# A delay in the written order for the small matmuls of the weight chains, and priority for the reductions behind them

## The chip, the cores and the metric

The kernel runs on 1 core of one Trainium2 chip. The metric is device microseconds of one execution, as the median of several runs. The core has five engines that are met here: TensorE (PE in the profile; its weight loads are PEld), VectorE (DVE), ScalarE (ACT), GpSimd (POOL) and SyncE (SP), which issues most DMAs. Each executes its own list of instructions in order, and semaphores tie the lists together.

## The reference, cut to what matters

A trunk of two layers over 2048 tokens plus 16 meta tokens of width 1024, in float32. Each layer is one input projection, attention in two groups of 8 heads, a gate, an output projection, and a layer norm of the residual sum:

```
x <- LayerNorm(alpha * x + (concat(heads_a, heads_b) * silu(gate)) @ w_out)
layer 0: stick-breaking attention (8 heads)  ||  multi-head latent attention (8 heads, rotary key)
layer 1: sliding-window attention with sinks ||  forgetting attention (8 heads)
stick-breaking: w[q,k] = exp(log_sigmoid(z[q,k]) + sum of log_sigmoid(-z[q,j]) over k < j < q)
```

The kernel works with pairs of float16 numbers (a high and a low part) in place of float32. To split a tensor that way it needs a power of two as its scale, and for the scale the largest absolute value of the tensor. To scale the mixed outputs it also needs bounds, and for those the largest norm of a column (of x and of some weights).

## The kernel before

**Stages.** Stick-breaking attention for 4 pairs of heads comes first, then latent attention for 4 pairs, the first output projection with its layer norm, forgetting attention for 4 pairs, sliding-window attention for 4 pairs, and the second output projection. Tokens are handled in 4 blocks of 512 and in tiles of 128. For each pair and block, a group of P blocks projects k, q, v and gate (`mm3` at L825 for k and q, `proj_4` at L915 for v and gate, `proj_tok` at L888 for the meta tokens). A blocks do the attention of a tile: scores by `qk` (L1087) into two PSUM banks, the softmax or the stick-breaking scans (L1415, L1417) and products (L1431), a split into high and low (L1205, L1218), a transpose by DMA (L588), the product with v (L1278 to L1280) into `psO`, and the multiplication with gate and factor (L1364 in the stick-breaking attention). F blocks do the output projections.

**The order.** The order of all instructions is written when the program is built, by a small event simulation (`Flow`). It has a clock `t`, a priority queue for each engine, and events. `f.job(engine, ns, fn, then, pr)` queues a step with an assumed duration; when the engine is free in the simulation, the job with the smallest `pr` is taken and `fn` writes its instructions; `then` is called after the duration and an assumed latency. Without `pr`, the priority is the time of queueing. `EARLY` and `LATE` are 3000 ns each: `f.t - EARLY` goes ahead of what has been waiting for less than that, `f.t + LATE` yields. `f.at(lag, fn)` calls `fn` after `lag` ns of simulated time. TensorE's queue (`"P"`) is emptied whenever the drive loop comes back to it, before the next few projection or score matmuls. On the chip, each engine executes what was written, in that order, whenever its operands are there.

**The weight chains.** `prep` loads a group of weights (two staging buffers, `wst`), takes the largest absolute value of each partition (L698), and calls `allreduce` for the largest over all partitions: VectorE writes a diagonal matrix of the 128 values (L626), TensorE multiplies it with ones (L631) so that each partition gets all values, VectorE reduces them (L634). The result becomes the scale (L86 to L90), and the group is split (L655 on ScalarE, L653 on VectorE or L645 and L646 on GpSimd) into one of four weight buffers (`wg`). For v and gates, `maxnorm` follows: squares (L755, on GpSimd, or for the parts of x mostly on VectorE), a matmul with ones that sums them (L760), a copy into a column (L781, L783), `allreduce`, and a square root (L790). The squares have one buffer (`nsq`), which is given back in `red`, right after the matmul has been placed. The norm of x takes 17 parts of up to 128 tokens through that buffer, one after the other; the norms of v and g of the first pair stand behind them in the same queue.

**What waits for the results.** A projection waits for its split weights. A norm group's weight buffer is given back when its norm is known. In the stick-breaking attention `pr.fm`, which L1364 needs, is computed when the norms of x, v and g are there (`units` in `phase_sb`). PSUM has 6 banks for scores and projections, at most 4 of them for scores, reductions and norms together ("S"); scores of a tile take two at once, and start when two are to be had. `psO` has two more buffers.

Of the kernel before, what the change touches and what calls it, by code (L numbers as in the profile page):

```python
# [16 lines left out]
ALU = mybir.AluOpType  # L17
AX = mybir.AxisListType
PSUM = bass.MemoryType.PSUM

D = 1024
# [18 lines left out]
EARLY, LATE, SLACK = 3000.0, 3000.0, 5000.0  # L40
XPOOL = (1, 4, 6)
NEGD = True
SWABIAS = 0.0
LOBIAS = 1000.0
MORE = ()
WGS = 4
SB_BYTES, MLA_ROWS, FOX_ROW = 204768, 24704, 8256
# [357 lines left out]
def dve(n):  # L405
    return 1.042 * n + 69.0


def gps(n):
    return 1.88 * n + 150.0  # L410
# [15 lines left out]
class Kern:  # L426
# [189 lines left out]
    def allreduce(self, m, then, pr=None):  # L616


        nc, f = self.nc, self.f
        r = self.small.tile([128, 1], F32, name="amr", tag="amr")  # L620

        def diag():
            d = self.small.tile([128, 128], BF16, name="amd", tag="amd", bufs=2)

            def fn():
                nc.vector.tensor_scalar(d, self.idbf, m, 1.0 + 2.0 ** -8, ALU.mult, ALU.mult)  # L626

            f.job("D", 190.0, fn, lambda: self.bk.get(lambda ps: ones(d, ps)), pr)

        def ones(d, ps):  # L630
            f.job("P", 60.0, lambda: nc.tensor.matmul(ps[:, :128], lhsT=self.ones, rhs=d, start=True, stop=True), lambda: red(ps), pr)  # L631

        def red(ps):
            f.job("D", dve(128), lambda: nc.vector.tensor_reduce(r, ps[:, :128], axis=AX.X, op=ALU.max), lambda: [self.bk.free("S", ps), then(r)], pr)  # L634

        diag()

# [103 lines left out]
    def maxnorm(self, parts, g, after=None, facs=None):  # L741


        nc, f = self.nc, self.f
        mx = self.small.tile([128, 24], F32, name="nmx", tag="nmx", bufs=3)
        left = [len(parts)]

        def one(i, sq):
            src = parts[i]
            k, n = src.shape[1], src.shape[2]  # L750
            if len(parts) > 1 and i % 3:
                e, ns, eng = "D", dve(k * n / 2), nc.vector
            else:
                e, ns, eng = "G", gps(k * n), nc.gpsimd
            f.job(e, ns, lambda: eng.tensor_tensor(sq[:, :k, :n], src, src, ALU.mult), lambda: self.bk.get(lambda ps: mm(i, k, n, sq, ps)), f.t + LATE)  # L755

        def mm(i, k, n, sq, ps):
            def fn():
                for kt in range(k):
                    nc.tensor.matmul(ps[:n, 0:1], lhsT=sq[:, kt, :n], rhs=self.ones[:, 0:1], start=kt == 0, stop=kt == k - 1)  # L760

            f.job("P", k * 28.0, fn, lambda: red(i, n, ps, sq))

        def red(i, n, ps, sq):
            self.nsq.free(sq)

            def end():
                self.bk.free("S", ps)
                left[0] -= 1
                if left[0]:  # L770
                    return
                if len(parts) > 1:
                    f.job("D", 90.0, lambda: nc.vector.tensor_reduce(mx[:, 23:24], mx[:, :len(parts)], axis=AX.X, op=ALU.max), lambda: self.allreduce(mx[:, 23:24], root))
                else:
                    self.allreduce(mx[:, 0:1], root)

            def fn():
                if n < 128:
                    nc.vector.memset(mx[:, i:i + 1], 0.0)
                if facs:  # L780
                    nc.vector.tensor_scalar(mx[:n, i:i + 1], ps[:n, 0:1], facs[i][:n], facs[i][:n], ALU.mult, ALU.mult)  # L781
                else:
                    nc.vector.tensor_copy(mx[:n, i:i + 1], ps[:n, 0:1])  # L783

            f.job("D", 140.0 if facs else 70.0, fn, end)

        r = self.small.tile([128, 1], F32, name="nr", tag="nr")

        def root(m):
            f.job("G", 460.0, lambda: nc.gpsimd.tensor_tensor(r, m, self.half, ALU.pow), fin)  # L790

        def fin():
            def fn():
                g.nb = self.p2.mul(r, self.p2.inv(g.s), 1.02)
                g.nready = True
                if after:
                    after()
            f.job("D", 450.0, fn)

        for i in range(len(parts)):  # L800
            self.nsq.get(lambda sq, i=i: one(i, sq))
# [392 lines left out]
    def pv_hi(self, e):  # L1194
# [14 lines left out]
        def lo():  # L1209
            d, g = dve(w), gps(w)  # L1210
            if e.meta:
                d, g = d + dve(32), g + gps(32)
            onD = f.load["D"] + d + LOBIAS < f.load["G"] + g
            eng, name, ns = (nc.vector, "D", d) if onD else (nc.gpsimd, "G", g)
# [1531 lines left out]
    def phase_out0(self):  # L2746
# [5 lines left out]
        def mem():  # L2752
            wo = B(4, [2, 1024], F16)
            mt = B(2, [8, 128], F16)
            for b in MORE:
                getattr(self, b).grow(1)
# [708 lines left out]
```

## Time and profile before

| | us |
|---|---|
| median of 3 runs (3091.64 to 3104.94) | 3101.06 |
| the profiled execution, own time | 3114.27 |
| its span | 3112.2 |
| TensorE busy (34,261 matmuls) | 2608.2 (84%) |
| VectorE busy | 2439.8 (78%) |
| ScalarE busy | 1775.4 (57%) |
| GpSimd busy | 1576.6 (51%) |

The span goes from the first to the last of the 88,537 instructions in the profile. Busy shares are averages over stages with different limits, and an engine that waits for a semaphore is not busy. Times in the rows below are microseconds from the start of the span, of this one execution; "idle" of an engine is put down to the instruction that released the next one.

### The profile page before, as it was taken

How to read it: one execution, taken by the hardware profiler on the slowest of the kernel's cores; microseconds unless marked ns; L12 is line 12 of the kernel's file. 1: busy time of each engine (PE TensorE's matmuls, PEld its weight loads, DVE VectorE, ACT ScalarE, POOL GpSimd, SP SyncE). 2: the span in 40 equal slices, each digit the busy share in tenths (PEclk: the TensorE clock that was granted, in tenths of full speed). 3: DMA queues.
4: the chain of work that ended last, by engine and by line, in shares of the span. 5: the costliest groups of instructions: out<-in, count | busy, mean ns of one | idle time of the engine just before them, and what ended most of it. 6: DMA issues, size and time to landing. Idle time of an engine off the chain costs nothing. (4 is left out here: it accounts for less than half of the span.)

```text
span 3112.2 us, 88537 instructions
## 1 busy us (share of the span) xinstructions
PE 2608.2 (84%) x34261; PEld 1794.9 (58%) x34261; DVE 2439.8 (78%) x6874; ACT 1775.4 (57%) x4082; POOL 1576.6 (51%) x2292
## 2 busy tenths in 40 slices
PE   4888988888887798888776799968969797799998
PEld 2676766766775455545554355646746465566643
DVE  8889899989998786667686875866757576588866
ACT  4667677757875465556575335455465554566611
POOL 3566566755754354445465534344454443456500
PEclk9989999999998999999887899989989899899999
DMA  4365465666798699999999985777667666555863
GB/s 153 54 125 108 98 120 113 114 115 108 128 162 186 166 196 215 221 212 188 164 166 168 215 205 87 145 134 141 115 125 134 118 128 107 101 123 100 177 166 112
DMA packets 1206808, 444.62 MB, mean 143 GB/s; under 512 B 1091616, under 2 KB 1171584, under 8 KB 1206384
## 3 DMA queue, kind: packets, MB, share of 16 engines
q1 hardware_dynamic: 1204048, 430.50, 71.1%
q0 software_dynamic: 2336, 8.46, 0.8%
q8 instruction: 268, 4.39, 0.6%
q14 instruction: 156, 1.28, 0.1%
HBM read 119.62 MB, written 51.06 MB: 55 GB/s over the span
## 5 line engine op out<-in xcount | busy, mean ns | idle before, releaser
L1218 POOL TENSOR_TENSOR mem<-mem 128x512 f16<-128x512 f32 (+3 forms) x751 | 823.6, 1107 | 440.4 <-ACT mem L1205 414.1
L825 PE MATMUL bank<-mem 128*128 128x512 f16 (+2 forms) x4272 | 929.1, 369 | 8.7 <-DVE mem L1485 2.6
L1205 ACT CAST mem<-mem 128x512 f16<-128x512 f32 (+3 forms) x1080 | 520.3, 513 | 276.6 <-DMA mem<-mem 134.4
L825 PEld LDWEIGHTS <-mem 128*128 128x128 f16 (+1 forms) x4272 | 405.9, 100 | 438.6 <-issue 88.2
L1278 PE MATMUL psO<-mem 128*128 128x64 f16 x3264 | 403.8, 200 | 294.4 <-DMA mem<-mem 287.8
L915 PE MATMUL bank<-mem 128*128 128x128 f16 x9984 | 643.7, 221 | 5.5 <-DVE mem L970 4.1
L915 PEld LDWEIGHTS <-mem 128*128 128x128 f16 x9984 | 578.3, 99 | 49.4 <-issue 41.0
L1087 PE MATMUL bank<-mem 64*128 64x256 f16 (+8 forms) x6264 | 521.3, 286 | 47.4 <-DVE mem L1431 22.5
L1278 PEld LDWEIGHTS <-mem 128*128 128x128 f16 x3264 | 307.4, 101 | 426.9 <-DMA mem<-mem 367.0
L1522 ACT ACTIVATE mem<-mem,smt,p 128x656 f32<-128x656 f32 (+16 forms) x264 | 336.3, 1275 | 237.3 <-DVE smt L1519 206.7
L1280 PE MATMUL psO<-mem 128*128 128x64 f16 x3264 | 400.6, 199 | 0.0
L1279 PE MATMUL psO<-mem 128*128 128x64 f16 x3264 | 400.5, 199 | 0.0
L1087 PEld LDWEIGHTS <-mem 64*128 64x128 f16 (+1 forms) x6264 | 271.8, 96 | 195.8 <-issue 100.1
L1279 PEld LDWEIGHTS <-mem 128*128 128x128 f16 x3264 | 310.3, 102 | 15.2 <-issue 2.4
L1280 PEld LDWEIGHTS <-mem 128*128 128x128 f16 x3264 | 311.1, 102 | 0.0
L1218 DVE TENSOR_TENSOR mem<-mem 128x512 f16<-128x512 f32 (+3 forms) x329 | 254.8, 791 | 66.4 <-ACT mem L1205 62.9
L1417 DVE TENSOR_TENSOR_SCAN mem<-mem 128x513 f32<-128x513 f32 (+2 forms) x224 | 290.7, 1325 | 4.9 <-ACT mem L1407 4.6
L1550 POOL TENSOR_TENSOR ist<-ist,p 128x2 f32<-128x2 f32 (+1 forms) x196 | 49.7, 254 | 425.1 <-DVE ist L1547 406.1
L1490 DVE CUSTOM_DVE_ANT_0 mem<-bank,mem 128x256 f32<-128x256 f32 (+6 forms) x484 | 195.5, 455 | 74.2 <-PE bank L1093 48.9
L1407 ACT ACTIVATE mem<-bank,p 128x512 f32<-128x512 f32 (+3 forms) x360 | 213.1, 592 | 45.0 <-PE bank L1087 44.4
L1325 POOL TENSOR_TENSOR mem<-mem 128x128 f16<-128x128 f32 (+1 forms) x264 | 136.9, 522 | 176.1 <-ACT mem L1322 174.3
L1485 DVE TENSOR_SCALAR_CACHE_REDUCE mem<-bank 128x512 f32<-128x512 f32 (+5 forms) x372 | 188.8, 545 | 38.3 <-PE bank L1093 22.6
(191 smaller groups left out, 4130.2 us busy)
## 6 DMA issues: line engine op xcount, KB each, us to landing
mem<-in_w_dram SPq DMA_DIRECT2D x46, 512.0 KB, 4.0
tmp_mx_dram<-mem SPq DMA_DIRECT2D x128, 128.0 KB, 2.4
mem<-in_wout_dram SPq DMA_DIRECT2D x32, 512.0 KB, 4.3
mem<-mem SPq DMA_TRANSPOSE x988, 3.4
mem<-tmp_cqT_dram SPq DMA_DIRECT2D x12, 1024.0 KB, 6.5
mem<-in_xr_dram SPq DMA_DIRECT2D x16, 512.0 KB, 4.5
tmp_res_dram<-mem POOLq DMA_DIRECT2D x16, 512.0 KB, 5.0
mem<-tmp_res_dram SPq DMA_DIRECT2D x16, 512.0 KB, 5.3
```

The source lines that it names most:

```text
L825: nc.tensor.matmul(out, lhsT=st(kt, a), rhs=mv(kt, b), start=i == 0 and j == 0, stop=i == m - 1 and j == 2)
L915: nc.tensor.matmul(ps[:, 128 * i:128 * i + 128], lhsT=mv(a)[:, kt, 128 * i:128 * i + 128], rhs=w[b][:, kt, c0:c0 + 128], start=i == 0 and ...
L1087: nc.tensor.matmul(o, lhsT=l, rhs=m, start=i == 0, stop=mask is None and i == len(run) - 1)
L1205: nc.scalar.copy(t[:r, a:a + w], e.P[:r, e.pcol:e.pcol + w])
L1218: eng.tensor_tensor(t[:r, a + w:a + 2 * w], e.P[:r, e.pcol:e.pcol + w], t[:r, a:a + w], ALU.subtract)
L1278: nc.tensor.matmul(out, lhsT=p[:, a, :r], rhs=vt[:, hd, 0, :], start=e.first and i == 0 and hd == 0, stop=False)
L1279: nc.tensor.matmul(out, lhsT=p[:, a, :r], rhs=vt[:, hd, 1, :], start=False, stop=False)
L1280: nc.tensor.matmul(out, lhsT=p[:, b, :r], rhs=vt[:, hd, 0, :], start=False, stop=False)
L1407: nc.scalar.activation(b[:r, 1:n + 1], ps[:r, :n], AF.Sigmoid, scale=pr.scn[:r])
L1417: nc.vector.tensor_tensor_scan(pc[:r, :n + 1], b[:r, :n + 1], self.diag[:r, :n + 1], prev[0], ALU.mult, ALU.bypass)
L1490: nc.vector.tensor_tensor_reduce(row[:r, o + oo:o + oo + w], ps[:r, oo:oo + w], pr.cum[kb][hd][:r, ko:ko + w], 1.0, -3e38, ALU.add, ALU.ma ...
L1522: nc.scalar.activation(row[:r, :n], row[:r, :n], AF.Exp, bias=st[:r, 1:2], scale=sc[:r], accum_out=it.st[:r, hd:hd + 1])
```

## The change

Three places change. In `allreduce`, the ones matmul is asked for 2500 ns of simulated time (`PESLACK`) after its diagonal instead of at once, and so is the PSUM bank that it takes; in `maxnorm`, the norm matmul likewise after its squares. The reduction behind the ones matmul (L634) gets priority `f.t - EARLY` instead of that of its chain, and so does the copy behind the norm matmul (L781, L783), which had the time of its queueing. All callers of `allreduce` and `maxnorm` are concerned: the weights, x, the weights of latent attention and of the output projections, and the layer-norm bounds.

```diff
+PESLACK = 2500.0
...
@@ allreduce
-            f.job("D", 190.0, fn, lambda: self.bk.get(lambda ps: ones(d, ps)), pr)
+            f.job("D", 190.0, fn, lambda: f.at(PESLACK, lambda: self.bk.get(lambda ps: ones(d, ps))), pr)
...
-            f.job("D", dve(128), lambda: nc.vector.tensor_reduce(r, ps[:, :128], axis=AX.X, op=ALU.max), lambda: [self.bk.free("S", ps), then(r)], pr)
+            f.job("D", dve(128), lambda: nc.vector.tensor_reduce(r, ps[:, :128], axis=AX.X, op=ALU.max), lambda: [self.bk.free("S", ps), then(r)], f.t - EARLY)
...
@@ maxnorm
-            f.job(e, ns, lambda: eng.tensor_tensor(sq[:, :k, :n], src, src, ALU.mult), lambda: self.bk.get(lambda ps: mm(i, k, n, sq, ps)), f.t + LATE)
+            f.job(e, ns, lambda: eng.tensor_tensor(sq[:, :k, :n], src, src, ALU.mult), lambda: f.at(PESLACK, lambda: self.bk.get(lambda ps: mm(i, k, n, sq, ps))), f.t + LATE)
...
-            f.job("D", 140.0 if facs else 70.0, fn, end)
+            f.job("D", 140.0 if facs else 70.0, fn, end, f.t - EARLY)
```

## Rows read from the trace of the kernel before

**Rows 1.** Stage: busy PE, PEld, DVE, ACT, POOL (xcount), PEclk, DMA share, GB/s.

```profile
131.00:165.00 34.00, 29.86 (x415) 20.35 (x415) 31.25 (x49) 25.44 (x60) 23.80 (x23) 0.95 0.73 133
165.00:200.00 35.00, 29.81 (x505) 25.99 (x503) 29.42 (x56) 23.77 (x53) 22.63 (x23) 0.90 0.54 86
...
300.00:350.00 50.00, 47.11 (x604) 33.26 (x602) 41.04 (x89) 28.20 (x72) 24.90 (x27) 1.00 0.39 84
350.00:1000.00 650.00, 550.77 (x8537) 429.62 (x8535) 612.39 (x1002) 472.33 (x1088) 412.82 (x423) 0.97 0.69 129
...
1060.00:1630.00 570.00, 466.63 (x6145) 294.37 (x6146) 406.88 (x1346) 348.97 (x805) 297.59 (x482) 0.93 1.02 195
...
1720.00:1785.00 65.00, 49.31 (x220) 20.93 (x218) 61.90 (x107) 22.98 (x21) 44.55 (x26) 0.87 0.93 207
1785.00:1805.00 20.00, 17.20 (x90) 9.74 (x90) 10.47 (x24) 6.79 (x9) 1.49 (x2) 0.84 0.57 163
1805.00:1850.00 45.00, 42.82 (x247) 20.81 (x245) 42.17 (x96) 12.65 (x13) 24.46 (x17) 0.99 0.93 227
1850.00:2850.00 1000.00, 847.50 (x11841) 604.19 (x11839) 703.08 (x2768) 546.09 (x1308) 469.93 (x851) 0.93 0.67 122
```

**Rows 2.** Line L631: until when TensorE idled before it (us, times).

```profile
  DVE amd L626: 73.5, 30
```

**Rows 3.** TensorE waits in 0:131, 1000:1060, 1630:1720, 1720:1850, 1850:2850: us, times, longest.

```profile
PE bank L631 <- DVE amd L626: 40.3, 8, 15.1
...
PE bank L631 <- DVE amd L626: 3.0, 1, 3.0
...
PE bank L631 <- DVE amd L626: 5.9, 2, 4.3
...
PE bank L631 <- DVE amd L626: 11.8, 5, 3.0
PE bank L760 <- POOL mem L755: 4.5, 1, 4.5
...
PE psO L1278 <- DMA mem<-mem: 123.3, 82, 8.8
PE bank L631 <- DVE amd L626: 8.6, 10, 1.5
```

**Rows 4.** Timeline of TensorE, 40 to 54 us: start, us, instruction.

```profile
53.30 0.26 PE L631 MATMUL bank<-amd,ones 128*128 128x128 bf16 x1 [7.21 <-DVE amd L626]
53.36 1.06 PE L825 MATMUL bank<-mem 128*128 128x512 f16 x2
```

**Rows 5.** Timeline: norm matmuls of x (first, 17th), of g; reduction of x.

```profile
68.61 0.34 PE L760 MATMUL bank<-ones,mem 128*128 128x1 bf16 x8
...
101.27 0.35 PE L760 MATMUL bank<-ones,mem 128*128 128x1 bf16 x8 [0.25 <-DVE mem L755]
...
106.89 0.22 PE L631 MATMUL bank<-amd,ones 128*128 128x128 bf16 x1
...
110.73 0.34 PE L760 MATMUL bank<-ones,mem 128*128 128x1 bf16 x8
...
113.18 0.28 DVE L634 TENSOR_REDUCE amr<-bank 128x1 f32<-128x128 f32 x1
```

**Rows 6.** Timeline of scores, last product; all of line L1364 (first and last start).

```profile
129.43 0.50 PE L1087 MATMUL bank<-mem 64*128 64x272 f16 x5 [0.93 <-DVE mem L1431]
...
137.44 0.83 PE L1087 MATMUL bank<-mem 64*128 64x384 f16 x12
...
139.20 0.78 DVE L1431 TENSOR_TENSOR mem<-bank,mem 128x272 f32<-128x272 f32 x2
...
L1364 DVE SCALAR_TENSOR_TENSOR mem<-psO,p,mem x68: 314/331/352, 131.5 to 1006.5; 128x128 f32<-128x128 f32 x64, 16x128 f32<-16x128 f32 x4
```

**Rows 7.** Line L970 (evacuations of q and k) in 131 to 165 us.

```profile
131.00:165.00 34.00, 1.46 (x2) 0.95 0.73 133
```

**Rows 8.** VectorE waits in 131 to 1000 us: us, times, longest.

```profile
DVE amr L634 <- PE bank L631: 5.5, 2, 4.9
```

## Prediction

> **What bounds the kernel now.** I read the page first. Over the whole span no engine is full, and averages over stages with different limits bound nothing, so I went to the table by stage [rows 1]. The reader is to see there that the bound changes. In the stick-breaking attention (131 to 1000 us) VectorE is busy 31.2 of 34, 29.4 of 35, 41.0 of 50 and 612 of 650 us: it sets the pace, and a microsecond in which it has nothing to do is lost unless a later gap takes it up. In the latent attention (1060 to 1630 us) the DMA share is 1.02. In the first output projection with its layer norm (1720 to 1850 us) VectorE is again nearly full, 61.9 of 65 and 42.2 of 45 us, except for 20 us in between (10.5, TensorE 17.2). In the forgetting attention (1850 to 2850 us) TensorE is highest, with 85%.
>
> Then the instructions that the change touches. The matmuls with ones (L631) found TensorE idle and waiting for their diagonal (L626) 30 times, 73.5 us in all [rows 2]. The view of waits, cut by stage, says where [rows 3]: 40.3 us of it lie before 131 us, 3.0 between 1000 and 1060, 5.9 between 1630 and 1720, 11.8 (and 4.5 of the norm matmuls L760) between 1720 and 1850, 8.6 from 1850 to 2850 us. The last row shows what stands behind them there: 123.3 us of waits for transposes (L1278).
>
> **What the change does, part by part.** No instruction is added or removed; three kinds of step move in the written order of their engines. The program's own clock only sets that order: the chip does not wait for 2.5 us, it executes whatever was placed in between.
>
> *The ones matmul and the norm matmuls 2.5 us later on TensorE.* A matmul whose operand is late stops the matmuls behind it. The clearest place is in the start: a ones matmul came at 53.30 us after 7.21 us of idling, and a projection starts 0.06 us behind it [rows 4]; how much of the 7.21 us it could have used, the rows do not say. With the change some 2.5 us of other matmuls stand before the ones. The mean wait is 73.5 / 30 = 2.45 us, so the usual one goes and the long ones (15.1, 7.2, 4.5, 4.3) are only shortened. What the waits are worth differs by stage:
>
> - Before 131 us: 0 to -7. I count 0, because the norm of x, below, sets the end of this stage.
> - 131 to 1000 us: 0, VectorE is the bound. The Trainium skill, "Perfetto Trace Analysis", section "Identifying Performance Opportunities", says to work on the most contended engine of a regime; for this stage it speaks against the change, and the row agrees with 612 of 650 us.
> - 1000 to 1060 us: between 0 and -3; TensorE's work is needed soon there, -2.
> - 1630 to 1720 us: between 0 and -6; half, -3.
> - 1720 to 1850 us, 16.3 us: VectorE has 3 us to spare in each of the two full stretches and 9.5 in the one between; -7, between 0 and -16.
> - 1850 to 2850 us, 8.6 us: behind these waits TensorE meets the transposes, fourteen times as much; a third, -3.
>
> *The norm of x, a serial chain.* This is the part that I weigh most. The norm of the input has 17 parts, and each holds the one buffer for squares (nsq) until its matmul has been placed; so the parts go one after the other. The first matmul is at 68.61 us and the 17th at 101.27 us, 32.7 / 16 = 2.04 us a part; the norms of v and g follow in the same line, g's at 110.73 us [rows 5]. With 2.5 us more in each part the 17th comes 17 x 2.5 = 42 us later, and g's 5 us more. TensorE and VectorE have other work through this stretch, so the delay is real in their orders.
>
> Who waits: a factor fm needs the norms of x, v and g, and every output tile of the stick-breaking attention is multiplied by it (L1364). The first is at 131.5 us, 20.8 us after g's norm matmul. Scores (L1087) had stopped at 129.43 us and go on at 137.44 us [rows 6]: the buffers between scores and output are full, so the attention can't run further ahead of fm than it does now. Reductions with priority give back about 5 us (the one of x waited from 106.89 to 113.18 us [rows 5]) and a VectorE with little else to do some 6 more. First L1364: 131.5 + 42 + 5 - 11 = about 168 us, +36.
>
> What that costs on VectorE, the bound: between 131 and 165 us it does 31.2 us [rows 1]. The evacuations of q and k are 1.46 us of that [rows 7]; with those of v and gates and the splits of weights I take 5 us for all that isn't attention. So 26 us of attention in 34, or 28 in 36, are missing. Off go 7 us of scans and products of scores made before the stop (the last product is over at 139.98 us [rows 6]); 2 us of evacuations for projections that TensorE does ahead in the meantime; and 9 us of VectorE's idling in 300 to 350 us (50 - 41.0), where TensorE is at 94% with the next pair's projections, which would now be further on. Remains **+10 us**. Bounds: 0, if the 5.6 us of idling in 165 to 200 us and later gaps take up the rest; +36, if nothing is made up.
>
> *Reductions with priority.* They free a PSUM bank sooner: the ones of x held theirs from 106.89 past 113.18 us [rows 5], one of four for scores, which are taken in pairs. No row prices a bank. The nearest is the 5.5 us in which VectorE waited for these matmuls [rows 8]; under a full VectorE a held bank costs little, later it may: -3, between 0 and -6. The same row prices the other side: a reduction placed right behind its matmul finds TensorE late, as it did once for 4.9 us. With less cover between the two I add +3, between 0 and +8.
>
> Sum: +10 + 3 - 2 - 3 - 7 - 3 - 3 = -5 us against the profiled execution of 3114.3 us (its span of 3112.2 us and 2.1 around it), 3109.3. That execution is 13.2 us above the median of the runs, 3101.06 us; so the forecast is **3096 us**. What a measurement can tell from no change is about 0.5%, 15.5 us: below 3085.6 or above 3116.6 us.
>
> **Rivals.**
> *The late first output is not made up.* The 36 us end up in the span: +36 + 3 - 18 = +21, 3122 us, slower. For it: VectorE is 94% full in 350 to 1000 us, so there is little to absorb with. Against it: 9 and 5.6 us of idling soon after. It decides as soon as the stick-breaking attention ends more than 18 us later than now (its last L1364 is at 1006.5 us [rows 6]), and can be measured from about 33 us.
>
> *Every wait of the chains turns into time.* 3.0 + 5.9 + 16.3 + 8.6 = 33.8 us after 1000 us: 3077 us with the +10 us of the first output, 3067 us if that is made up. For it: TensorE is at 85% in the two longest stages. Part of it could be the clock: the granted clock is 0.87 in 1720 to 1785 and 0.84 in the 20 us after it, where TensorE idles before these matmuls, against 0.99 in 1805 to 1850 us, where it is busy 42.8 of 45 us [rows 1]. The missing shares are 0.13 x 65 + 0.16 x 20 = 11.7 us at the level of 2.4 GHz. The Trainium skill, "TensorE: Matmul & The Clock Gate", section "HAM oscillation — how this bites in real kernels", says that idle gaps put the engine back to half rate; by that rule these 11.7 us come back together with the gaps, and the time would be 3065 us. Against this rival: VectorE at 95% in two of those three stretches, and the transposes.
>
> *The change doesn't do what it says.* VectorE is behind the written order by more than 2.5 us, the waits stay and only move. For it: the waits of 4.3, 4.5 and 7.2 us. Then the order is reshuffled without a direction: 3101 us, give or take 10.
>
> **Chances.** Forecast (3086 to 3107 us) 0.32; every wait turns into time 0.34; the delay is not made up, or only half, 0.24; no effect 0.10. All of the 88,537 instructions behind the first moved one can shift against each other, and in each case I allow 10 us either way for that. Range 3060 to 3125 us: from the second rival to the first. Faster by over 0.5%: 0.36 (the second rival and a tail of the forecast); within: 0.41; slower: 0.23.
>
> **What would show it.** In the new profile the waits of L631 for L626 after 131 us fall from 33 us (73.5 - 40.3) to under 12. The 17 norm matmuls of x end near 144 us instead of 101; the first L1364 comes near 168 us, and VectorE idles 15 us or more between 131 and 170 us. The last L1364 comes some 10 us later than 1006.5 us. The stretch of 1720 to 1850 us shrinks by about 7 us. The prediction is wrong if the first L1364 stays near 131 us (the time is then below 3090 us), or if VectorE idles over 25 us more than now before 1000 us (then above 3115 us).

## The result and the profile after

The changed kernel takes 3121.03 us (median of 4 runs, 3118.33 to 3125.75), the kernel before in the same session 3102.18 us. The ratio is 1.0055, with a 95% interval of 1.0033 to 1.0077: slower by some 17 us, where 3096 us and no measurable change were forecast. The profiled execution took 3120.66 us, with a span of 3118.8 us; that of the kernel before (3114.27 us) was 12 us above its median, so the two traces lie only 6 us apart. All lines from L45 on stand one lower than before (L631 is now L632, L1364 is L1365).

More than half of the waits at which the change aims went away. The first fence is TensorE's idling before the ones matmul over the whole span (us, times), then the waits of TensorE in 0 to 131 us.

```profile
  DVE amd L627: 32.3, 7
```

```profile
PE bank L632 <- DVE amd L627: 26.6, 3, 14.3
```

Of the 73.5 us in 30 waits [rows 2] 32.3 in 7 are left, and 26.6 of these lie before 131 us. Behind it remain 5.7 us, where there were 33.2.

The norm matmuls of x, from the timeline of TensorE: the first, the sixth, the seventh, the twelfth and the 17th.

```profile
68.37 0.34 PE L761 MATMUL bank<-ones,mem 128*128 128x1 bf16 x8
...
95.61 0.34 PE L761 MATMUL bank<-ones,mem 128*128 128x1 bf16 x8
...
104.67 0.34 PE L761 MATMUL bank<-ones,mem 128*128 128x1 bf16 x8
...
146.29 0.34 PE L761 MATMUL bank<-ones,mem 128*128 128x1 bf16 x8
...
169.02 0.34 PE L761 MATMUL bank<-ones,mem 128*128 128x1 bf16 x8
```

The chain starts where it did and ends 68 us later, at 169.02 instead of 101.27 us [rows 5]. Who waits for it, line L1365 with its first and last start:

```profile
L1365 DVE SCALAR_TENSOR_TENSOR mem<-psO,p,mem x68: 318/338/353, 191.8 to 1039.0; 128x128 f32<-128x128 f32 x64, 16x128 f32<-16x128 f32 x4
```

The first output tile comes 60 us later than before, the last 32.5 us later [rows 6]. By stage, in the columns of [rows 1]:

```profile
131.00:165.00 34.00, 33.46 (x518) 28.40 (x513) 24.68 (x48) 12.21 (x20) 7.27 (x5) 1.00 0.14 41
165.00:200.00 35.00, 32.63 (x410) 24.50 (x408) 23.62 (x61) 8.97 (x17) 14.01 (x15) 0.95 0.33 67
300.00:350.00 50.00, 42.27 (x734) 36.71 (x732) 48.40 (x85) 36.22 (x73) 32.42 (x30) 0.97 0.67 100
350.00:1000.00 650.00, 550.05 (x8463) 422.79 (x8461) 614.00 (x1018) 475.97 (x1116) 425.80 (x429) 0.96 0.71 131
...
1729.00:1859.00 130.00, 111.28 (x588) 53.56 (x587) 117.83 (x227) 43.19 (x43) 61.93 (x39) 0.89 0.84 209
```

Three things are to be seen against [rows 1]. VectorE now idles 20.7 of the 69 us from 131 to 200 us (69 - 24.68 - 23.62), before 8.3. The gap at 300 to 350 us, where it had idled 9, is used to the last 1.6 us, as the prediction had it. And the projection of the outputs got no clock back. It comes 9 us later here (L2679 first at 1723.0 us, before L2678 at 1714.1), so its stretch of 130 us starts at 1729 us, and the granted clock in it is 0.89. It was 0.91 in 1720 to 1850 us of the kernel before:

```profile
1720.00:1850.00 130.00, 109.33 (x554) 51.49 (x553) 114.54 (x226) 42.42 (x43) 70.49 (x43) 0.91 0.87 207
```

The waits of TensorE there, the same two lines for 1720 to 1850 and for 1729 to 1859 us:

```profile
PE bank L761 <- POOL mem L756: 13.0, 2, 11.6
...
PE bank L632 <- DVE amd L627: 2.3, 1, 2.3
```

The 11.8 us behind diagonals [rows 3] fell to 2.3, but a norm matmul now waits 11.6 us for its squares on GpSimd; the sum is 15.3 instead of 16.3 us.

### The profile page after: what moved, and what is told of

The parts are those of the page before. It is cut to its first block, busy times and chain, and to the rows that moved or that the text cites. A ratio compares the mean times of both kernels' runs of the same rounds, so it can differ in the third digit from the quotient of the medians.

```text
span 3118.8 us, 88540 instructions
## 1 busy us (share of the span) xinstructions
PE 2625.6 (84%) x34261; PEld 1808.3 (58%) x34261; DVE 2440.2 (78%) x6899; ACT 1770.0 (57%) x4082; POOL 1548.6 (50%) x2267
## 5 line engine op out<-in xcount | busy, mean ns | idle before, releaser
L1219 POOL TENSOR_TENSOR mem<-mem 128x512 f16<-128x512 f32 (+3 forms) x741 | 806.0, 1098 | 437.2 <-ACT mem L1206 391.5
L1279 PE MATMUL psO<-mem 128*128 128x64 f16 x3264 | 408.5, 201 | 307.6 <-DMA mem<-mem 299.4
L1088 PE MATMUL bank<-mem 64*128 64x256 f16 (+8 forms) x6264 | 527.7, 288 | 54.4 <-DVE mem L1432 23.5
L1280 PE MATMUL psO<-mem 128*128 128x64 f16 x3264 | 405.2, 200 | 0.0
L1281 PE MATMUL psO<-mem 128*128 128x64 f16 x3264 | 405.1, 200 | 0.0
L1280 PEld LDWEIGHTS <-mem 128*128 128x128 f16 x3264 | 313.6, 103 | 18.2 <-issue 4.3
L1219 DVE TENSOR_TENSOR mem<-mem 128x256 f16<-128x256 f32 (+3 forms) x339 | 257.6, 777 | 57.8 <-ACT mem L1206 55.8
```

Source lines behind the costliest of these rows:

```text
L1088: nc.tensor.matmul(o, lhsT=l, rhs=m, start=i == 0, stop=mask is None and i == len(run) - 1)
L1219: eng.tensor_tensor(t[:r, a + w:a + 2 * w], e.P[:r, e.pcol:e.pcol + w], t[:r, a:a + w], ALU.subtract)
L1279: nc.tensor.matmul(out, lhsT=p[:, a, :r], rhs=vt[:, hd, 0, :], start=e.first and i == 0 and hd == 0, stop=False)
L1280: nc.tensor.matmul(out, lhsT=p[:, a, :r], rhs=vt[:, hd, 1, :], start=False, stop=False)
L1281: nc.tensor.matmul(out, lhsT=p[:, b, :r], rhs=vt[:, hd, 0, :], start=False, stop=False)
```

## The experiments

Theory 1: the serial chain of x, whose parts are each asked for 2.5 us later, costs the time. Theory 2: the loss comes from the other moves. Each kernel was timed beside the kernel before, whose medians in the five sessions were 3103.5 to 3106.6 us; the ratio is to that, with its 95% interval.

**The delay of x's parts taken out, or made alone.**

Only x has more than one part. The first edit is made in the changed kernel (x_parts_no_slack), the second is all that is changed in the kernel before (x_parts_only).

```diff
-f.at(PESLACK, lambda: self.bk.get(lambda ps: mm(i, k, n, sq, ps)))
+f.at(PESLACK if len(parts) == 1 else 0.0, lambda: self.bk.get(lambda ps: mm(i, k, n, sq, ps)))
...
-self.bk.get(lambda ps: mm(i, k, n, sq, ps))
+f.at(PESLACK if len(parts) > 1 else 0.0, lambda: self.bk.get(lambda ps: mm(i, k, n, sq, ps)))
```

Expected without the delay of x:

> The change as it is, but the 17 norm matmuls of x are asked for at once, without the 2.5 us. Theory 1 (the serial norm chain of x alone costs the time: it ended at 169 us instead of 101): the first output tile of the stick-breaking attention falls from 191.8 back to about 131 to 140 us, the last one from 1039 to about 1006 us, and the time to 3085 to 3103 us, at or a little under the kernel before (3102). Theory 2 (the loss comes from the other moves, the ones matmuls of the weights and the reductions with priority, behind which VectorE and GpSimd wait longer than before): the first output tile comes early again but the time stays above 3112 us.

Expected with it alone:

> The kernel before with one thing from the change: 2.5 us before each of the 17 norm matmuls of x. Theory 1: the first output tile comes near 185 us and the time is 3118 to 3130 us, so the whole loss or more of it. Theory 2: the late first output is made up before the end, and the time is within 3095 to 3108 us.

Measured: 3103.11 us without it (1.0002, 0.9988 to 1.0016), 3126.32 us with it alone (1.0089, 1.0068 to 1.0109). The line of the output tile, first of the one and then of the other kernel:

```profile
L1365 DVE SCALAR_TENSOR_TENSOR mem<-psO,p,mem x68: 314/336/354, 151.3 to 1001.1; 128x128 f32<-128x128 f32 x64, 16x128 f32<-16x128 f32 x4
```

```profile
L1365 DVE SCALAR_TENSOR_TENSOR mem<-psO,p,mem x68: 313/335/352, 184.1 to 1041.4; 128x128 f32<-128x128 f32 x64, 16x128 f32<-16x128 f32 x4
```

This is as theory 1 has it, and everything in the change besides x's parts is worth nothing (-4 to +5 us). That the output still came at 151.3 us, and not by 140 as expected, cost nothing either.

**The other moves alone.** `ones_slack_only` is the kernel before with the delay in `allreduce` only; `priority_only` is the change with `PESLACK = 0.0`.

> The kernel before with 2.5 us before the ones matmuls of the largest values alone; no delay of norm matmuls, no priority for reductions. Theory 1: the waits of the ones matmuls after 131 us go (33 us to under 12) and the time is 3090 to 3103 us, the first output tile within 10 us of 131.5. Theory 2: above 3108 us. If the time is within 5 us of the kernel before while the waits are gone, the waits were not on the path that sets the end.

> The change with the delay at 0: only the priority of the reductions and copies remains. Theory 1: 3095 to 3106 us, nothing that can be told from the kernel before, the waits of the ones matmuls still near 70 us in all. Theory 2: a part of the loss, 3108 us or more.

Measured: 3108.12 us (1.0022, 1.0008 to 1.0035) and 3104.54 us (1.0003, 0.9989 to 1.0016). Neither gives the loss, but the first fits neither theory well: it is 5 us above the range of theory 1 and just at the bound of theory 2, its first output came at 147.8 us, and it is no faster although the waits are down to 27.2 us in all.

**A late factor by itself.** In the kernel before, only the job that computes the first pair's `fm` is queued D later:

```diff
-lambda: f.job("D", 1200.0, fin))
+lambda: f.at(D if pr.i == 0 else 0.0, lambda: f.job("D", 1200.0, fin)))   # D = 20000, 50000, 60000, 66000, 70000
```

> The kernel before, in which nothing of the change is made; only the job that computes the factor fm of the first pair is put 20 us of simulated time later. This prices a late first output by itself. The prediction's sum (a late first output of 36 us costs 10 us, so that the first 26 are made up): the first output tile near 151 us, the time within 3100 to 3108 us. Rival (nothing is made up): about 20 us more, 3120 us or above.

> The same with 50 us. The first output tile comes near 180 us, as late as in the kernel with the delay in the parts of x alone (184.1 us, 3126.3 us). If the lateness of fm is the whole loss, the time is 3118 to 3130 us; if the serial chain costs something besides (VectorE's and GpSimd's squares in the middle of the attention), it is under 3115 us. By the prediction's price (the part beyond 26 us is lost) it would be some 24 us over the kernel before, 3128 us.

> The kernel before with the job of the first factor alone 70 us of simulated time later, so that the first output comes near 195 us, later than in the changed kernel (191.8), while all norms and weight buffers are on time. Theory F: 3112 to 3130 us. Theory W: 3098 to 3109 us.

> The kernel before with the first factor 60 us of simulated time later, between 50 us (first output 175.1, 3101 us) and 70 us (199.6, 3142 us). Theory of the cliff (until about 175 us VectorE has other work to do, the next pair's weights and projections, that it need not do later; then it runs dry, and each further microsecond of lateness ends up in the time): first output near 187 us, VectorE idle 15 to 18 us of the 35 in 165 to 200 us, 3108 to 3125 us. Rival (the price jumps with the order that happens to come out, not with the lateness): 3095 to 3105 us, or above 3130 us.

> The kernel before with the first factor 66 us later, between 60 us (first output 190.1, 3107 us) and 70 us (199.6, 3142 us). If there is a point from which a late factor is lost: 3112 to 3140 us. If the 3142 us were the order's: 3100 to 3110 us.

Measured: 20 us 3103.91 (1.0001, 0.9988 to 1.0014), 50 us 3100.99 (0.9993, 0.9977 to 1.0009), 60 us 3106.74 (1.0011, 1.0000 to 1.0021), 66 us 3141.70 (1.0111, 1.0093 to 1.0129), 70 us 3142.32 (1.0117, 1.0098 to 1.0135). The first output came at 148.7, 175.1, 190.1, 196.6 and 199.6 us. So 50 us of lateness are free, 60 cost 3 us and 66 cost 35. The prediction's own price (3128 us at 50 us) falls; 60 us came out between the ranges of its two cases, 66 and 70 us somewhat above the ranges of theirs. The stage of 131 to 200 us shows the stock that makes it free, for 50 us and then for 66 us:

```profile
131.00:165.00 34.00, 30.58 (x389) 22.30 (x388) 31.76 (x60) 17.00 (x31) 12.62 (x12) 1.00 0.21 64
165.00:200.00 35.00, 32.20 (x583) 28.95 (x581) 23.87 (x54) 17.25 (x41) 14.15 (x17) 1.00 0.67 118
```

```profile
131.00:165.00 34.00, 30.57 (x375) 21.71 (x373) 32.01 (x56) 19.46 (x37) 14.46 (x14) 1.00 0.17 48
165.00:200.00 35.00, 33.94 (x500) 29.31 (x497) 16.63 (x53) 6.79 (x13) 5.65 (x7) 1.00 0.26 69
```

Until 165 us VectorE is as busy as in the kernel before (31.8 and 32.0 of 34 us), with the next pair's weights in place of a part of the attention: at 66 us the lines L653 and L698 take 11.0 us there, before 3.1, and scans and products (L1415, L1417, L1431) 16.2, before 24.5. Behind that it runs dry, and in 165 to 200 us idles 11.1 us at 50 us of delay and 18.4 us at 66. What it waits for in that stretch of the latter is the rest of this work: gates from ScalarE, the split halves, the weights' loads:

```profile
DVE mem L1771 <- ACT mem L1770: 8.3, 2, 4.6
DVE mem L653 <- ACT mem L655: 5.1, 1, 5.1
DVE wmm L698 <- DMA mem<-in_w_dram: 1.7, 2, 1.4
```

But the kernel with 60 us idles as long there (18.2 us) and loses 3 us. The two differ little in their last output tile of the stick-breaking attention (1049.9 and 1055.3 us), and much in the first of the latent attention, L1563, for 60 and then for 66 us:

```profile
L1563 DVE TENSOR_TENSOR mem<-psO,mem x196: 268/288/293, 1064.5 to 2955.1; 128x128 f32<-128x128 f32 x192, 16x128 f32<-16x128 f32 x4
```

```profile
L1563 DVE TENSOR_TENSOR mem<-psO,mem x196: 267/286/293, 1095.6 to 2993.3; 128x128 f32<-128x128 f32 x192, 16x128 f32<-16x128 f32 x4
```

Where exactly the step lies is thus also a matter of the order that comes out; what made these 31 us was not taken apart.

**What stands behind the parts in the queue.** The norms of v and gates follow x's parts, and hold three weight buffers until they are known. `weights_first` is the whole change with these norms put to the front of the queue for `nsq`; `norms_late_50` is the kernel before with the last job of the first pair's norms 50 us later.

```diff
-self.nsq.get(lambda sq, i=i: one(i, sq))
+fn = lambda sq, i=i: one(i, sq)
+if len(parts) == 1 and f.t < 3.0e5:
+    self.nsq.q.appendleft(fn)
+    self.nsq.pump()
+else:
+    self.nsq.get(fn)
...
-f.job("D", 450.0, fn)
+if any(g is w for w in self.sbp[0].g.values()):
+    f.at(50000.0, lambda: f.job("D", 450.0, fn))
+else:
+    f.job("D", 450.0, fn)
```

> The whole change, but up to 300 us of simulated time the norms of weights (v, gates) go to the front of the queue for the squares' buffer, ahead of the parts of x that still wait. The late factor by itself was free (50 us: 3101 us), so two theories are left for the loss of the delayed chain of x. Theory W (what stands behind the 17 parts in the queue: the norms of v and of the gates, without which three of the four weight buffers are not given back, so that the next pair's weights can't be split in the hole): the first output stays late (180 us or later), the third and fourth largest value of the next pair's weights come before 175 us instead of at 186 and 229, and the time is 3100 to 3110 us. Theory F (the factor is later than in that run, 192 against 175 us, past what can be made up): 3115 us or more.

> The kernel before with the last job of the norms of v and of both gates of the first pair 50 us of simulated time later; x's chain is not touched. The factor is late by this, and the three weight buffers are held as long. Theory W: 3112 to 3128 us. Theory F, by which holding the buffers costs nothing beside the late factor (first output near 175 us, which was free): 3097 to 3107 us.

Measured: 3123.37 us (1.0064, 1.0041 to 1.0086) with the first output at 200.3 us, and 3111.80 us (1.0016, 1.0003 to 1.0028) at 174.8 us. Theory W falls by the first: the third and fourth largest value of the next pair's weights (L699) came at 159.9 and 163.7 us, as early as it asked, and the time did not fall to 3110 us. The second lies between the ranges of the two theories; held for long the buffers cost some 5 us, by the interval at most 9.

**Why a part takes 6.3 us.** `x_squares_prompt` is the whole change with another priority for the squares of x, `half_slack` with another delay.

```diff
-f.t + LATE)
+f.t + (LATE if len(parts) == 1 else 0.0))
...
-PESLACK = 2500.0
+PESLACK = 1250.0
```

> The whole change, but the squares of the parts of x are queued at the time of their asking and do not yield for 3 us. This tests why a part took 6.3 us instead of 2.04 + 2.5 = 4.5. Theory A (the squares yield to the attention that has begun meanwhile, so that the late chain makes itself later): a part takes 3.5 to 4.7 us, the 17th norm matmul comes by 145 us, the first output near 165 us, the time is 3103 to 3114 us. Theory B (the rest of a part is waiting on TensorE's and GpSimd's lists): a part stays near 6 us, the first output near 190 us, the time near 3120 us.

> The whole change with a delay of 1.25 us in place of 2.5. The 17th norm matmul of x comes near 130 us, before the attention stops for the factor for long; both theories: first output 150 to 165 us, 3098 to 3110 us. If the loss goes with the length of the delay it is half, about 3112 us.

Measured: 3120.79 us (1.0046, 1.0027 to 1.0064) and 3115.38 us (1.0036, 1.0021 to 1.0052), first output 184.7 and 166.2 us. The 17th norm matmul of the two, from the timelines:

```profile
166.29 0.34 PE L761 MATMUL bank<-ones,mem 128*128 128x1 bf16 x8
```

```profile
149.87 0.34 PE L761 MATMUL bank<-ones,mem 128*128 128x1 bf16 x8
```

Theory A falls: without the yielding a part still takes (166.29 - 68.22) / 16 = 6.1 us. With half the delay it takes 5.1 us, not 3.3, and the time is above what either theory gave (3098 to 3110 us, or about 3112).

**What a reshuffled order is worth, and the late stages.** `slack_100_ns` and `slack_300_ns` are the whole change with `PESLACK` at 100 and 300. `late_stages_only` makes the four edits of the change depend on the simulated time, `output_only` the same with `1.0e6 < f.t < 1.8e6`. `x_parts_2300_ns` is x_parts_only with 2300.

```diff
+f.at(PESLACK if f.t > 1.0e6 else 0.0, lambda: self.bk.get(lambda ps: ones(d, ps)))
...
+f.t - EARLY if f.t > 1.0e6 else pr
```

> The whole change with a delay of 0.1 us in place of 2.5: next to nothing is moved, but the order behind it comes out another way than with the delay at 0, which took 3104.5 us. It measures what a reshuffled order alone is worth. If single differences of 4 to 9 us between the kernels of this study are worth reading one by one: within 3 us of 3104.5. If they are the lottery of the order: 4 us or more away from it, either way.

> The same with 0.3 us; the chain of x gets at most 17 x 0.3 = 5 us longer, far from the cliff. Same two cases: within 3 us of 3104.5, or 4 us and more away.

> The change, delay and priority, from 1000 us of simulated time on, which leaves the stick-breaking attention as in the kernel before and takes in everything from the weights of the first output projection on. It asks what the waits of the chains behind 1630 us are worth, 5.9 + 16.3 + 8.6 = 30.8 us in the kernel before. If they are on the path that sets the end, as the prediction's sum has it with 13 of them: 3088 to 3095 us. If what stands behind them (transposes, VectorE) takes their place: within 4 us of the kernel before, with the waits of the ones matmuls in these stages under 8 us.

> Delay and priority only between 1000 and 1800 us of simulated time, so for the weights of the first output projection and the start of the forgetting attention; nothing else is changed. The prediction gave these stages -3 and -7 us (of 5.9 and 16.3 us of waits). If the waits of the ones matmuls there are worth what it says: 3090 to 3098 us. If a wait of the norm matmul for GpSimd's squares takes their place (13.0 us of it in the changed kernel in 1720 to 1850 us, 4.5 before): 3102 us or more, and that wait is there again.

> As the kernel before with the delay in the 17 parts of x alone, with 2.3 us in place of 2.5: the same cause, another order behind it. The chain is 3.4 us shorter, which is nothing beside its 68; but a 0.1 us delay moved the whole time by 14 us, so a single order proves little. If the delayed chain is the cause of the loss: 3116 us or more again (3126 with 2.5 us). If the loss was a lottery of the order: within 3095 to 3112 us.

Measured: 0.1 us of delay 3119.39 us (1.0055, 1.0033 to 1.0076), 0.3 us 3091.67 us (0.9960, 0.9944 to 0.9975), late stages 3111.44 us (1.0027, 1.0012 to 1.0042), output projection 3111.85 us (1.0023, 1.0009 to 1.0037), 2.3 us in x alone 3110.73 us (1.0015, 0.9999 to 1.0032). A delay of 0, 0.1 and 0.3 us gives +0.03, +0.55 and -0.40%: a reordering without a direction is worth as much as the change. The late stages alone come out 8 us slower than the kernel before, neither faster nor within the 4 us expected. In output_only the wait that took the place of the others is there again:

```profile
PE bank L761 <- POOL mem L756: 11.9, 2, 10.5
...
PE bank L632 <- DVE amd L627: 2.3, 1, 2.3
```

And 2.3 us in x's parts gave no second loss of the size, which by its expectation speaks for the lottery of the order; but its chain ended at 161.01 us and the first output came at 174.8 us, on the free side. So a single kernel proves little here, and the runs are read as two groups, by the first output tile:

| first output | kernels (first output us, ratio) | mean ratio |
|---|---|---|
| 131 to 175 us | late_stages 131.2 1.0027, output 131.4 1.0023, priority 137.4 1.0003, slack_300 137.7 0.9960, ones 147.8 1.0022, fm_20 148.7 1.0001, x_no_slack 151.3 1.0002, slack_100 155.4 1.0055, half 166.2 1.0036, norms 174.8 1.0016, x_2300 174.8 1.0015, fm_50 175.1 0.9993 | 1.0013 |
| 184 to 200 us | x_only 184.1 1.0089, squares 184.7 1.0046, fm_60 190.1 1.0011, the change 191.8 1.0055, fm_66 196.6 1.0111, fm_70 199.6 1.0117, weights_first 200.3 1.0064 | 1.0070 |

Up to 175 us there is no clear trend. Beyond 184 us the mean is 0.57% higher, 18 us, and five of seven lie at or above the highest of the first group. The border between the groups was drawn after the results were known.

**Where the time is lost.** The first output tile of the latent attention parts the stick-breaking attention from all that follows. It is L1563 in the kernel before (first line), L1564 in the changed one (second) and in late_stages_only (third). That last kernel gives VectorE and ScalarE the same instructions in the same order as the kernel before until 1629 us:

```profile
L1563 DVE TENSOR_TENSOR mem<-psO,mem x196: 268/288/293, 1068.1 to 2961.7; 128x128 f32<-128x128 f32 x192, 16x128 f32<-16x128 f32 x4
```

```profile
L1564 DVE TENSOR_TENSOR mem<-psO,mem x196: 253/287/293, 1077.6 to 2963.1; 128x128 f32<-128x128 f32 x192, 16x128 f32<-16x128 f32 x4
```

```profile
L1564 DVE TENSOR_TENSOR mem<-psO,mem x196: 269/286/293, 1059.1 to 2946.3; 128x128 f32<-128x128 f32 x192, 16x128 f32<-16x128 f32 x4
```

In output_only, with the same order up to there, the tile comes at 1060.0 us. Against these two executions (3104.8 and 3107.5 us, near the median of the kernel before) the changed kernel is 18 us late at this point, as much as it loses in all. From there to the end of the span it takes 2041.2 us, the three others 2044.1, 2043.9 and 2045.6 us. The groups say the same: the twelve kernels reach this point at 1058.2 us on average, the seven at 1078.7 us, with one profiled execution each, and the seven are not slower behind it. So the loss is made in the stick-breaking attention. That holds for slack_100_ns too (1072.9 us), whose first output was on time: an unlucky order can lose as much in the same stage.

## Why the prediction was wrong

Its sum was +10 for x's late norm and -15 for all the rest. Measured were about +17 and nothing.

**The chain of x, mis-sized.** The prediction had 17 x 2.5 = 42 us, the 17th norm matmul near 144 us and the first output near 168 us; they came at 169.02 and 191.8 us. "With 2.5 us more in each part" took the 2.04 us of a part as given. In the five steps to 95.61 us a part takes 5.4 us, in the six steps to 146.29 us 8.4, in the last five 4.5, the predicted number. The six long steps lie where the attention has begun and VectorE is full (28.40 of 31 us in 100 to 131 us), the last five where it has stopped for the factor. One of the long ones, on VectorE between the matmuls at 127.64 and 135.69 us:

```profile
127.42 1.46 DVE L1418 TENSOR_TENSOR_SCAN mem<-mem 128x273 f32<-128x273 f32 x2
...
130.14 0.27 DVE L782 TENSOR_SCALAR nmx<-bank,p 128x1 f32<-128x1 f32 x1
130.32 0.91 DVE L1219 TENSOR_TENSOR mem<-mem 128x256 f16<-128x256 f32 x1
...
131.73 0.68 DVE L756 TENSOR_TENSOR mem<-mem 128x1024 bf16<-128x1024 f16 x1
```

The next square starts 4.1 us after the matmul that freed its buffer, behind scans, products and splits of the attention, and its own matmul 3.3 us after its end. A delayed chain runs into work that it had been ahead of. That the meeting adds to the delay shows where there is next to none: with 0.1 us, in slack_100_ns, eleven steps take 2.7 us up to 97.30 us, then five 6.0 (to 127.34 us), and in x_parts_no_slack the last two take 6.0 and 8.9 us (94.69 to 109.55 us). The squares' yielding isn't it (x_squares_prompt); that it is the place in the written lists of the engines is the reading left over, and no run took it apart further.

**The price of a late first output, mis-sized.** "Remains +10 us" let 26 of the 36 us be made up and lost the rest one for one, with bounds of 0 and +36; by that rule the 60 us that came would have cost 34. The runs make up more, and then look like a step: some 45 us are free, as at 175.1 us (0.9993), and beyond about 184 us 18 us are lost on average, up to 36. At the forecast's own 168 us the loss would have been no more than what the order moves: half_slack at 166.2 us and x_2300 at 174.8 us, with ratios of 1.0036 and 1.0015, lie within the first group. The mechanism, with the gap at 300 to 350 us filled, was right; the lateness that can be made up was larger than thought, and the lateness larger still. That the stock of work done ahead sets the point is argued from the two stages of 131 to 200 us, not shown.

**VectorE's idling as the measure.** "Wrong if VectorE idles over 25 us more before 1000 us (then above 3115)": it is busy 911.22 us before 1000 us, before 924.25, so it idles 13 us more, and the time is above 3115 us all the same. The mark at 1000 us cuts through a stage that ends at different times. Taken up to the first output tile of the latent attention, with the same matmuls done, the kernel before, the changed one and late_stages_only have:

```profile
0.00:1068.10 1068.10, 878.45 (x12895) 671.12 (x12896) 971.25 (x1747) 706.43 (x1592) 625.23 (x635) 0.96 0.62 123
```

```profile
0.00:1077.60 1077.60, 889.17 (x12895) 678.32 (x12896) 968.12 (x1749) 703.04 (x1591) 621.34 (x633) 0.95 0.63 122
```

```profile
0.00:1059.10 1059.10, 874.21 (x12894) 668.10 (x12895) 969.68 (x1746) 704.66 (x1591) 630.55 (x635) 0.97 0.62 124
```

VectorE is busy for nearly the same time in all three, and idles 97, 109 and 89 us. The 20 us between the last two are about the loss. So idle time of VectorE was the right measure for this stage; its end and its threshold of 25 us were not.

**The gains of -15 us.** The terms were -2, -3, -7 and -3 for waits, -3 for banks, +3 for prompt reductions. The waits fell as foreseen (33.2 to 5.7 us behind 131 us, under the 12 that the prediction had set), but x_parts_no_slack, which holds all of these terms, gained nothing, nor did the kernels with the ones matmuls, the late stages or the output projection alone (1.0022, 1.0027, 1.0023). In 1720 to 1850 us a norm matmul waits for its squares instead, 15.3 us of waits in place of 16.3. For the other stages no run shows the reason; waits that go without time coming back were presumably not on the path that sets the end. How many us they are worth can't be told more closely than the 0.4% or so by which a reshuffled order moves the time.

**The rivals.** "The late first output is not made up" gave 3122 us, and its condition (the last output over 18 us later) was met with 32.5 us; but it lost part of 60 us where it had counted all of 36, so that its number agrees with the time is luck. "Every wait turns into time" is out: neither time nor clock came back (granted clock 0.931 in the profiled execution, before 0.940). Nor does the clock carry the loss: with the delay of x's parts taken out and with it alone it is 0.936 in both profiled executions, 23 us apart in their medians. "Does not do what it says" is out for the waits. The allowance of 10 us either way for the shifted order was too small: 17 us up and 12 down were seen.

**What stays open.** Why 60 us of pure lateness cost 3 us and 66 us 35, other than that the difference is there when the latent attention starts; whether the change's own 17 us are the step or partly the order's, since a single kernel (slack_100_ns) has the same ratio without the late output. The pair with the delay of x's parts taken out and made alone points the same way as the two groups, and the groups carry the cause; no single pair does. The kernel with the least time, slack_300_ns, beats both, and by the same argument is a lucky order and no design.

## What to carry to other kernels

A delay that takes a wait off one instruction is paid once for each link of a serial chain: before it is put into a helper, list its callers, and leave out those that run the helper many times through one buffer. Ask what work the delayed chain will meet at its new place, and how much other work the engine has in stock for the hole; here some 45 us of lateness were free, and beyond some 60 they were not. In a kernel whose order is written by a simulation, measure first what a change of no meaning does to the time, here 0.4 to 0.5%, and judge groups of variants rather than one.

## What the runs showed of the hardware

A diagonal of the norms takes 451 ns on average in the kernel before and 736 ns in the changed one, the same instruction with the same operands. First before, then after:

```profile
L626 DVE TENSOR_SCALAR amd<-idbf,nmx 128x128 bf16<-128x128 bf16 x30 | 13.4, 451 | 0.4
```

```profile
L627 DVE TENSOR_SCALAR amd<-idbf,nmx 128x128 bf16<-128x128 bf16 x30 | 22.1, 736 | 2.5 <-PE bank L632 2.2
```

The timeline of the changed kernel at 169 us shows one of them:

```profile
169.45 1.89 POOL L756 TENSOR_TENSOR mem<-mem 128x1024 bf16<-128x1024 f16 x1 [6.21 <-PE bank L761]
...
169.92 1.47 DVE L627 TENSOR_SCALAR amd<-idbf,nmx 128x128 bf16<-128x128 bf16 x1
```

The square on GpSimd lasts from 169.45 to 171.34 us, and the diagonal, which takes 0.25 us elsewhere (one for a weight at 187.23 us), from 169.92 to 171.39 us: it ends when the square does. The Trainium skill, "SBUF — State Buffer", section "Who interferes with whom", says that VectorE and GpSimd share one pair of ports, and that of two instructions that need it the later one waits until the earlier is done; these rows agree. The 30 diagonals cost VectorE 8.7 us more without doing more. Over all diagonals the sum is smaller: the 52 of the largest values of the weights (`wmm`) fell from 21.6 to 18.1 us in all. It is no part of the loss that can be seen, as VectorE's busy time up to the latent attention did not grow.
